# Hybrid encoder: the memory attention is issued after the first q tile, its values product in float32, and GpSimd makes the high parts of four w_out blocks

## The chip, the cores and the metric

The kernel runs on one core of one Trainium2 chip. The metric is the device time of one execution in microseconds. A core has a TensorE (PE, with its weight loads shown apart as PEld), a VectorE (DVE), a ScalarE (ACT), a GpSimd (POOL) and a SyncE (SP, which here issues most DMAs). Each engine works through its own instruction queue in order and waits on semaphores for the others.

## The reference

Two layers of an encoder on a sequence of 1024 rows of 1024 floats. In each layer three token mixers read one projection of the normed rows: a Fourier mixer, attention over a window of 128 to either side, and an attention of four heads over 256 memory rows. Their normed outputs go through `w_out`, and a gated feed-forward block follows.

```python
def _memory_attn(q, km, vm):
    scores = jnp.einsum('bshd,bmhd->bhsm', q, km).astype(jnp.float32) * (HEAD_DIM ** -0.5)
    probs = jax.nn.softmax(scores, axis=-1)
    return jnp.einsum('bhsm,bmhd->bshd', probs, vm).reshape(b, s, MEM_WIDTH)

for l in range(DEPTH):                                   # DEPTH = 2
    z = _rmsnorm(x, g_pre_mix[l]) @ w_in[l]              # (1024, 1024) @ (1024, 1280)
    zf, zq, zk, zv, zm = jnp.split(z, splits, axis=-1)   # 256, 512, 128, 128, 256
    y_f = _fourier_mix(zf, w_fourier[l])
    q = _rope(zq.reshape(b, s, 8, 64), positions)
    k = _rope(zk.reshape(b, s, 2, 64), positions)
    y_a = _window_attn(q, k, zv, sink[l])
    km, vm = jnp.split(_rmsnorm(mem, g_mem[l]) @ w_mem_kv[l], 2, axis=-1)   # 256 rows of memory
    y_m = _memory_attn(zm.reshape(b, s, 4, 64), km, vm)
    y = jnp.concatenate([_rmsnorm(y_f, ..), _rmsnorm(y_a, ..), _rmsnorm(y_m, ..)], -1) @ w_out[l]
    x = x + _rmsnorm(y, g_post_mix[l])
    gate, up = jnp.split(_rmsnorm(x, g_pre_ffn[l]) @ w_ffn_in[l], 2, axis=-1)
    x = x + _rmsnorm((jax.nn.silu(gate) * up) @ w_ffn_out[l], g_post_ffn[l])
```

The change touches the memory attention (`_memory_attn`) and the preparation of `w_out` for the product behind the three mixers.

## The kernel before, in words

**Products.** Nearly all matrix products are made in fp32r, with each operand split into a high part (a cast to fp32r, mostly on ACT) and a low part (what the cast left over, mostly a subtraction on DVE). A product is then three matmuls: high by high, high by low, low by high (`Acc.add`). `split` (L150 to L152) makes both parts of a tile.

**Memory.** Two large tiles are addressed in slots of 256 words per partition: `arena_r` for fp32r data and `arena_f` for float32, through `at(k, ...)`. `Ring` and `run` give several slots in turn. Weights that don't fit there lie in `big`, a pool of four buffers of 8 KB per partition. PSUM has four tags of two buffers each: `sc`, `pT`, `av`, `pd`.

**Stages of a layer's mixing part.** `zf` and the Fourier units; `kvz`, eight token tiles of 128 rows, that make keys, values and the memory queries (`zst`); `q`, eight token tiles: `q(t)` makes 24 matmuls of 512 columns (L162, tile `qp`) with the q weights, which fill the four `big` buffers, then the rotation (`rope`, DVE and POOL), and `q_turn(t)` transposes the result (L743, tile `qT`) and makes its high and low parts. `Memory.load` fetches the memory's keys and values, made earlier, from DRAM and splits them: `dup_stack` (L397 to L400) makes eight casts on ACT and eight subtractions on DVE for the keys.

**The memory attention** has 10 units for 8 pairs of a head and a half of the sequence. Unit i issues `mem_scores` of pair i: 16 matmuls of 256 columns (L873, tile `ms`), maxima on DVE (L875, L876), four exponentials on ACT (L879), a reciprocal on DVE (L883) and four multiplications on POOL (L885). It then issues `mem_values` of pair i - 2: four fp32r matmuls of 512 columns (L906, tile `mav`), whose 128 output rows are the 64 columns of the head by the high and by the low part of the values; ACT copies one half (L909) and DVE adds the other (L910). Last comes `mem_turn` of pair i - 1: eight transposes (L895, tile `mpT`) into two PSUM tiles, each split into high and low part (L151 on ACT, L152 on DVE).

**w_out.** `load_wout` takes eight raw blocks of 128 x 512 per call through a ring of three slots: a DMA (L942), the high part on ACT (L943), the low part on DVE (L944), for four row blocks. One call puts them into `big`, once the q weights are used up; the other puts them into `arena_r`. `fm_load` makes both, and `fm_units` the products of the Fourier and memory columns with them (tile `mo`, L162), whose sums go to DRAM until the last mixer is done. The windowed attention (`att_units`, tiles `sc`, `pT`, `av`) comes in two halves of the heads, and the second is woven with the rest of `w_out`. A feed-forward stage of Strassen-like blocks takes up the rest of the layer.

**Order.** The program is issued in the order of the Python code, where `weave` merges lists of units evenly; a scheduler then orders the instructions of each engine by their dependences and modelled times, so that the order on an engine isn't the order of the code. Buffers of pools may share memory where their uses don't overlap, and the later use waits for the earlier. In the main loop the q units 0 to 3 are issued first, then `mem.load()`, then the memory units woven with the q units 4 to 7, `fm_load` and the rest.

## Time and profile before

| what | value |
| --- | --- |
| median of 3 runs | 2080.04 us (2077.87 to 2081.79) |
| the profiled execution | 2080.67 us |
| its span, first to last instruction | 2078.9 us |
| mean granted TensorE clock | 0.981 |
| chain that ended last, by engine | PE 79%, DVE 7%, DMA 5%, ACT 3% |
| stage of the q tiles and the memory attention, layer 0 and layer 1 | 122.7 to 245 us, 1150.2 to 1260 us |

The span is that of one profiled execution, and all rows of the trace belong to it; its own time is 1.8 us longer, which lies outside the first and last instruction. The page gives busy shares over the whole span; the stage concerned is some 110 to 120 us long in each of the two layers. The slices of the page, each a fortieth of the span (52 us), show it as a dip of PE in slices 5 and 25, with DVE high at the same place:

```profile
PE   7998999799999999999999989998999999999998
PEld 6876787588888888887888768876888888878886
DVE  5668767898787886768876687679887787778766
```

A digit is the busy share of a slice in tenths. The trace also gives the busy times in any stretch, each engine's idle times with what ended them, and single instructions with start and length; rows of such views stand in the prediction.

### The profile page before, as it was taken

How to read it: one execution, taken by the hardware profiler on the slowest of the kernel's cores; microseconds unless marked ns; L12 is line 12 of the kernel's file. 1: busy time of each engine (PE TensorE's matmuls, PEld its weight loads, DVE VectorE, ACT ScalarE, POOL GpSimd, SP SyncE). 2: the span in 40 equal slices, each digit the busy share in tenths (PEclk: the TensorE clock that was granted, in tenths of full speed). 3: DMA queues.
4: the chain of work that ended last, by engine and by line, in shares of the span. 5: the costliest groups of instructions: out<-in, count | busy, mean ns of one | idle time of the engine just before them, and what ended most of it. 6: DMA issues, size and time to landing. Idle time of an engine off the chain costs nothing.

```text
span 2078.9 us, 28540 instructions
## 1 busy us (share of the span) xinstructions
PE 1996.4 (96%) x9587; PEld 1646.8 (79%) x9587; DVE 1572.7 (76%) x2540; ACT 1071.5 (52%) x2270; POOL 714.1 (34%) x819
## 2 busy tenths in 40 slices
PE   7998999799999999999999989998999999999998
PEld 6876787588888888887888768876888888878886
DVE  5668767898787886768876687679887787778766
ACT  7467777554333333545555677686433333345451
POOL 5344445433333433002423544453442342320012
PEclk9999999899999999999999999998999999999999
DMA  6112132423232333879741122233233233269983
GB/s 222 45 48 67 61 102 96 158 67 106 96 115 94 115 103 115 304 267 327 273 153 49 57 67 77 78 123 130 97 117 101 87 132 97 97 210 342 302 274 141
DMA packets 173347, 286.48 MB, mean 138 GB/s; under 512 B 15464, under 2 KB 73360, under 8 KB 173200
## 3 DMA queue, kind: packets, MB, share of 16 engines
q1 hardware_dynamic: 165136, 265.78, 38.4%
q10 hardware_dynamic: 8064, 18.88, 2.4%
q8 instruction: 75, 1.23, 0.2%
q14 instruction: 72, 0.59, 0.1%
HBM read 218.02 MB, written 66.58 MB: 137 GB/s over the span
## 4 chain that ended last, share of the span: by engine, by line
PE 79%; DVE 7%; DMA 5%; ACT 3%; issue 2%; POOL 2%; SPq 0%; DVEq 0%; POOLq 0%; ACTq 0%
PE fo L1272 14%; PE qx L1137 11%; PE qz L1137 11%; PE qy L1137 11%; PE mo L162 7%; PE qw L1137 6%; PE kvp L162 4%; PE qp L162 3%; DVE arena_r L152 2%; DMA arena_f<-actd 2%; PE pT L798 2%; PE zT L162 2%; PE sc L761 2%; DMA arena_f<-in_w_ffn_out 1%; PE av L813 1%
## 5 line engine op out<-in xcount | busy, mean ns | idle before, releaser
L151 ACT CAST arena_r<-arena_f 128x512 fp32r<-128x512 f32 (+1 forms) x780 | 443.8, 591 | 646.4 <-PE qz L1137 114.0
L152 DVE TENSOR_TENSOR arena_r<-arena_f,arena_r 128x512 fp32r<-128x512 f32 (+1 forms) x676 | 509.4, 775 | 146.3 <-ACT arena_r L151 136.4
L1272 PE MATMUL fo<-arena_r 128*128 128x512 f32 x1848 | 426.5, 392 | 8.1 <-ACT arena_r L151 6.9
L1272 PEld LDWEIGHTS fo<-arena_r 128*128 128x128 f32 x1848 | 347.9, 189 | 82.0 <-ACT arena_r L151 5.7
L1137 PE MATMUL qy<-arena_r 128*128 128x512 f32 x1056 | 261.6, 397 | 21.4 <-ACT arena_r L151 15.3
L1137 PEld LDWEIGHTS qy<-arena_r 128*128 128x128 f32 x1056 | 201.3, 192 | 66.1 <-ACT arena_r L151 16.4
L1127 DVE TENSOR_TENSOR arena_f<-arena_f 128x512 f32<-128x512 f32 x220 | 201.3, 920 | 11.5 <-DMA arena_f<-in_w_ffn_in 6.7
L1137 PE MATMUL qz<-arena_r 128*128 128x512 f32 x704 | 195.7, 389 | 0.2 <-ACT arena_r L151 0.2
L1157 POOL TENSOR_TENSOR arena_f<-arena_f 128x512 f32<-128x512 f32 x44 | 74.5, 1695 | 318.0 <-ACT arena_f L1142 318.0
L1137 PEld LDWEIGHTS qz<-arena_r 128*128 128x128 f32 x704 | 132.1, 188 | 28.0 <-ACT arena_r L151 0.6
L152 POOL TENSOR_TENSOR arena_r<-arena_f,arena_r 128x256 fp32r<-128x256 f32 (+2 forms) x104 | 86.3, 837 | 123.0 <-ACT arena_r L151 88.7
L1137 PE MATMUL qw<-arena_r 128*128 128x512 f32 x528 | 127.3, 389 | 0.0
L1137 PE MATMUL qx<-arena_r 128*128 128x512 f32 x528 | 127.3, 389 | 0.0
L1137 PE MATMUL qx<-big,arena_r 128*128 128x512 f32 x528 | 127.0, 389 | 0.0
L1189 POOL TENSOR_TENSOR arena_f<-arena_f 128x512 f32<-128x512 f32 x40 | 66.2, 1655 | 170.5 <-DVE arena_f L1169 127.1
L1137 PEld LDWEIGHTS qx<-arena_r 128*128 128x128 f32 x528 | 99.1, 188 | 20.6
L1137 PEld LDWEIGHTS qx<-big,arena_r 128*128 128x128 f32 x528 | 99.1, 188 | 20.6
L1137 PEld LDWEIGHTS qw<-arena_r 128*128 128x128 f32 x528 | 99.1, 188 | 20.6
L1137 PE MATMUL qz<-big,arena_r 128*128 128x512 f32 x352 | 115.2, 389 | 0.0
L210 POOL TENSOR_SCALAR rrsv<-rss 128x1 f32<-128x1 f32 x32 | 15.7, 492 | 268.1 <-ACT arena_f L323 208.6
L162 PE MATMUL mo<-big,arena_r 128*128 128x512 f32 x384 | 104.1, 410 | 0.7 <-ACT arena_f L1001 0.4
L162 PE MATMUL mo<-arena_r 128*128 128x512 f32 x384 | 100.5, 402 | 0.4 <-ACT arena_f L1001 0.3
(228 smaller groups left out, 3520.0 us busy)
## 6 DMA issues: line engine op xcount, KB each, us to landing
arena_f<-in_w_ffn_out SPq DMA_DIRECT2D x264, 256.0 KB, 4.7
arena_f<-in_w_ffn_in SPq DMA_DIRECT2D x88, 512.0 KB, 3.6
actd<-arena_f SPq DMA_DIRECT2D x154, 256.0 KB, 3.7
arena_f<-actd SPq DMA_DIRECT2D x154, 256.0 KB, 4.6
arena_f<-in_w_in SPq DMA_DIRECT2D x40, 256.0 KB, 2.9
arena_f<-in_x SPq DMA_DIRECT2D x16, 512.0 KB, 4.9
arena_f<-in_w_out SPq DMA_DIRECT2D x32, 256.0 KB, 2.8
pmd<-arena_f ACTq DMA_DIRECT2D x32, 256.0 KB, 2.0
```

The costliest lines, as they stand in the source:

```text
L151: nc.scalar.copy(hi, src)
L152: return (lo_eng or nc.vector).tensor_tensor(out=lo, in0=src, in1=f32(hi), op=ALU.subtract)
L162: mm(self.dst, a, b, start=self.i == 0, stop=self.i == self.n - 1)
L210: nc.gpsimd.tensor_scalar(out=v, in0=ss, scalar1=1.0 / n, scalar2=EPS, op0=ALU.mult, op1=ALU.add)
L761: mm(pt, lhs, self.kst[g][i][:, k0 * P : k1 * P], start=i == 0, stop=i == 1)
L798: nc.tensor.transpose(pT[:, h, :], es_[h // 2][:, h % 2, j * P : j * P + P], ident)
L813: mm(av, lhs, p_, start=j == 0 and i == 0, stop=j == nk - 1 and i == 1)
L1127: nc.vector.tensor_tensor(out=s, in0=a, in1=b, op=op)
L1137: mm(pt, a, b, start=start and n == 0, stop=n == 11, skip_group_check=not start)
L1157: nc.gpsimd.tensor_tensor(out=self.v, in0=self.v, in1=self.s2, op=ALU.add)
L1189: (G if i in (0, 3) else V).tensor_tensor(out=a[i], in0=c, in1=g[i], op=ALU.mult)
L1272: mm(pt, ab[:, 0, x, sl], ab[:, 1, y], start=new and first and j == 0, stop=last and j == 2, skip_group_check=not new)
```

## The change

Six edits:

- Slots 8 to 15 of the float32 arena become a tile of their own, `flex`, which is allocated anew as fp32r for the memory's keys when `mem.load()` is issued, and as float32 again when the windowed attention first writes its output there. Before, the keys lay in slots 16 to 23 of `arena_r`, where the normed rows of the first half lie until q tile 3 is done. The rings `es_ring` and `mps` get other slots.
- `mem.load` fetches keys and values in two DMAs; the values go straight to float32 slots and aren't split.
- `mem_turn` makes one float32 copy on ACT of each transposed tile in place of a high and a low part.
- `mem_values` works for a pair of heads: for each of two blocks of memory rows and each head one float32 matmul with 64 weight columns, into that head's half of the PSUM tile, and one copy on DVE. It is issued in units 3, 5, 7 and 9.
- `load_wout` fetches the left halves of its four row blocks before the right halves, and in the call into `big` POOL makes the high part.
- In the main loop only q unit 0 is issued ahead of `mem.load()`, and units 1 to 7 are woven with the memory units.

```diff
--- before.py
+++ after.py
@@ -88,8 +88,16 @@
 
     arenas = {
         F32R: cp.tile([P, ARENA_R * 256], F32R, name="arena_r"),
-        F32: cp.tile([P, ARENA_F * 256], F32, name="arena_f"),
+        F32: cp.tile([P, (ARENA_F - 8) * 256], F32, name="arena_f"),
     }
+    fxp = ctx.enter_context(tc.tile_pool(name="fxp", bufs=1))
+    flex = {}
+
+    def reflex(dt):
+        flex["t"] = fxp.tile([P, 8 * 256], dt, tag="flex", name=nm("flex"))
+        return flex["t"]
+
+    reflex(F32)
     bp = ctx.enter_context(tc.tile_pool(name="bp", bufs=4))
 
@@ -99,8 +107,11 @@
 
     def at(k, *shape, dt=F32):
 
+        t = arenas[F32R if dt is F32R else F32]
+        if dt is not F32R and k >= 8:
+            k, t = (k - 8, flex["t"]) if k < 16 else (k - 8, t)
         o = int(k * 256)
-        ap = arenas[F32R if dt is F32R else F32][:, o : o + math.prod(shape)]
+        ap = t[:, o : o + math.prod(shape)]
         return shaped(ap.bitcast(dt) if dt is I32 else ap, shape)
 
@@ -125,14 +136,14 @@
     raws, junks = run(0, 3, 2), Ring(56)
     yfs, turns, kvs, ds = run(8, 2, 1), Ring(32, 34), Ring(10, 56, 58), run(12, 2, 2)
     ropes = {2: run(6, 4, 0.5), 8: run(36, 6, 2)}
-    ems, es_ring, y1s = run(16, 4, 2), run(33, 5, 3), run(6, 2, 1)
+    ems, es_ring, y1s = run(16, 4, 2), Ring(36, 39, 42, 45, 33), run(6, 2, 1)
     sqs, pms, xfs = run(16, 2, 2), run(20, 2, 2), Ring(16, 20, 24, 28, 32, 0)
     qws, sns, silus, acts = Ring(32, 0, 16, 20), Ring(36, 38, 40, 42, 32, 34), run(8, 5, 2), run(18, 7, 2)
     sums, wsums = run(8, 4, 2), Ring(4, 6)
     ras, rbs, bsums, xs_ = run(40, 3, 2), run(46, 6, 2), Ring(58, 32, 34), Ring(36, 24)
 
     zzs, dhs, tabs = run(112, 2, 4), run(64, 2, 4), run(72, 4, 2)
-    mps, phs, yys = run(24, 2, 4), run(16, 3, 4), run(104, 2, 4)
+    mps, phs, yys = Ring(56, 58, 32, 34), run(16, 3, 4), run(104, 2, 4)
     wcs, abs_ = Ring(112, 116, 96, 100, 48, 52, 56, 60), Ring(80)
 
     def sm(n, name="v"):
@@ -471,16 +482,15 @@
             nc.sync.dma_start(kvd[self.l], at(self.ks, 1024))
 
         def load(self):
-            raw = at(32, 4, 256)
-            nc.sync.dma_start(raw, kvd[self.l].rearrange("p (i c) -> p i c", i=4))
-            self.km = [at(16 + 4 * i, 2, 2, NMEM, dt=F32R) for i in range(2)]
-            self.vm = at(120, 2, 4, 2, HD, dt=F32R)
+            raw = at(32, 2, NMEM)
+            nc.sync.dma_start(raw, kvd[self.l, :, 0:512].rearrange("p (i c) -> p i c", i=2))
+            self.v = at(6, 2, 4, HD)
+            nc.sync.dma_start(self.v, kvd[self.l, :, 512:1024].rearrange("p (t h d) -> p t h d", t=2, h=4))
+            km = shaped(reflex(F32R), (2, 2, 2, NMEM))
+            self.km = [km[:, i] for i in range(2)]
             for ci in range(2):
                 for j in range(2):
                     dup_stack(self.km[ci][:, j, 0], self.km[ci][:, j, 1], raw[:, ci], j)
-            v = raw[:, 2:4].rearrange("p t (h d) -> p t h d", h=4)
-            for mt in range(2):
-                split(self.vm[:, mt, :, 0, :], self.vm[:, mt, :, 1, :], v[:, mt])
 
 
     class Mix:
@@ -844,6 +854,7 @@
                     n = i - SKEW
                     half, c = divmod(n, 4)
                     if g == 0 and n == 0:
+                        reflex(F32)
                         ya = at(8, 2, 2, 512)
                         self.ya[0, 0], self.ya[0, 1] = ya[:, 0], ya[:, 1]
                     if g == 0:
@@ -893,21 +904,17 @@
                 pT = ps([4, P], "mpT", "pT")
                 for b in range(4):
                     nc.tensor.transpose(pT[:, b, :], e[b // 2][:, b % 2, mt * P : mt * P + P], ident)
-                pp = mps(2, 512, dt=F32R)
-                split(pp[:, 0], pp[:, 1], pT.rearrange("p h q -> p (h q)"))
-                res.append((pp[:, 0], pp[:, 1]))
+                pf = mps(512)
+                nc.scalar.copy(pf, pT.rearrange("p h q -> p (h q)"))
+                res.append(pf)
             return res
 
-        def mem_values(self, h, half, pp):
+        def mem_values(self, pr, half, pfs):
             av = ps([512], "mav", "av")
             for mt in range(2):
-                lhs = self.mem.vm[:, mt, h].rearrange("p a d -> p (a d)")
-                for i in range(2):
-                    mm(av, lhs, pp[mt][i], start=mt == 0 and i == 0, stop=mt == 1 and i == 1)
-            s = h % 2
-            d = self.ym[half][64 * s : 64 * s + 64, h // 2, :]
-            nc.scalar.copy(d, av[64:128])
-            nc.vector.tensor_tensor(out=d, in0=av[0:64], in1=d, op=ALU.add)
+                for s in range(2):
+                    mm(av[64 * s : 64 * s + 64], self.mem.v[:, mt, 2 * pr + s], pfs[s][mt], start=mt == 0, stop=mt == 1)
+            nc.vector.tensor_copy(self.ym[half][:, pr, :], av)
 
         def mem_units(self):
             todo = [(h, half) for half in range(2) for h in range(4)]
@@ -917,34 +924,35 @@
             def unit(i):
                 if i < n:
                     st[i] = self.mem_scores(*todo[i])
-                if i >= 2:
-                    h, half = todo[i - 2]
-                    if h == 0 and half == 0:
+                if i >= 3 and i % 2:
+                    h, half = todo[i - 3]
+                    if i == 3:
                         ym = at(24, 2, 2, 512)
                         self.ym = [ym[:, i] for i in range(2)]
-                    self.mem_values(h, half, pp.pop(i - 2))
+                    self.mem_values(h // 2, half, [pp.pop(i - 3), pp.pop(i - 2)])
                 if 1 <= i <= n:
                     pp[i - 1] = self.mem_turn(st.pop(i - 1))
 
             return [lambda i=i: unit(i) for i in range(n + 2)]
 
-
         def load_wout(self, ks, k0=None):
 
-            res = {}
-            for j, k in enumerate(ks):
-                w = big(2, D) if k0 is None else at(k0 + 8 * j, 2, D, dt=F32R)
-                hi, lo = w[:, 0], w[:, 1]
-                g = ggT[:, self.l * NK + k : self.l * NK + k + 1]
-                for n in range(2):
-                    ns = slice(n * 512, n * 512 + 512)
+            w = [big(2, D) if k0 is None else at(k0 + 8 * j, 2, D, dt=F32R) for j in range(len(ks))]
+            res = {k: (w[j][:, 0], w[j][:, 1]) for j, k in enumerate(ks)}
+            for n in range(2):
+                ns = slice(n * 512, n * 512 + 512)
+                for k in ks:
+                    hi, lo = res[k]
+                    g = ggT[:, self.l * NK + k : self.l * NK + k + 1]
                     raw = raws(512)
                     nc.sync.dma_start(raw, T["w_out"][self.l, k * P : (k + 1) * P, ns])
-                    nc.scalar.activation(hi[:, ns], raw, AF.Copy, scale=g)
+                    if k0 is None:
+                        nc.gpsimd.tensor_scalar(out=hi[:, ns], in0=raw, scalar1=g, scalar2=1.0, op0=ALU.mult, op1=ALU.mult)
+                    else:
+                        nc.scalar.activation(hi[:, ns], raw, AF.Copy, scale=g)
                     nc.vector.scalar_tensor_tensor(
                         out=lo[:, ns], in0=raw, scalar=g, in1=f32(hi[:, ns]), op0=ALU.mult, op1=ALU.subtract
                     )
-                res[k] = (hi, lo)
             return res
 
         def group_scale(self, parts, n, ring):
@@ -1364,10 +1372,9 @@
         kvz = mix.skewed(mix.kvz, mix.kvz_turn, NT)
         weave(mix.fourier_units(), kvz[:8] + [mix.q_load] + kvz[8:])
         q = mix.skewed(mix.q, mix.q_turn, NT)
-        for u in q[:4]:
-            u()
+        q[0]()
         mem.load()
-        weave(mix.mem_units(), q[4:8] + [mix.fm_load] + q[8:])
+        weave(mix.mem_units(), q[1:8] + [mix.fm_load] + q[8:])
         fm = mix.fm_units(pmd)
         weave(mix.att_units(0), fm[:6] + [mix.out_load] + fm[6:])
         mix.out_gains()
```

What this does to the order of the instructions is shown at three places, all in layer 0. A row is a line, an operation, the tile written and the tiles read, with the number of that allocation, the shape and a count of equal neighbours. Code lines of the changed program are some ten higher: L173 is L162, L884 is L873, L906 is L895, L408 to L411 are L397 to L400, and L952 and L953 are L943 and L944.

PE before, at the first scores of the memory attention; `qp_1497`, `qp_1598` and `qp_1728` are the q tiles 3, 4 and 5, `big_1305` to `big_1329` the four buffers with the q weights, `ms` the scores:

```order
L162 MATMUL qp_1497<-big_1329,arena_r 128x512 x6
L162 MATMUL qp_1598<-big_1305,arena_r 128x512 x3
L873 MATMUL ms_1571<-arena_r 128x256 x3
L873 MATMUL ms_1580<-arena_r 128x256 x3
L162 MATMUL qp_1598<-big_1305,arena_r 128x512 x3
L162 MATMUL qp_1598<-big_1313,arena_r 128x512 x2
L743 MATMUL qT_1529<-const,arena_f 128x128 x4
L162 MATMUL qp_1598<-big_1313,arena_r 128x512 x4
L162 MATMUL qp_1598<-big_1321,arena_r 128x512 x6
L162 MATMUL qp_1598<-big_1329,arena_r 128x512 x6
L162 MATMUL qp_1728<-big_1305,arena_r 128x512 x4
```

PE of the changed program, at its first scores; `qp_1889` and `qp_1969` are q tiles 6 and 7, `big_1309` to `big_1333` the q weights, `flex_1421` the keys:

```order
L173 MATMUL qp_1889<-big_1325,arena_r 128x512 x6
L173 MATMUL qp_1889<-big_1333,arena_r 128x512 x6
L173 MATMUL qp_1969<-big_1309,arena_r 128x512 x6
L173 MATMUL qp_1969<-big_1317,arena_r 128x512 x6
L173 MATMUL qp_1969<-big_1325,arena_r 128x512 x6
L173 MATMUL qp_1969<-big_1333,arena_r 128x512 x6
L884 MATMUL ms_1450<-flex_1421,arena_r 128x256
L884 MATMUL ms_1459<-flex_1421,arena_r 128x256
L884 MATMUL ms_1450<-flex_1421,arena_r 128x256 x3
L884 MATMUL ms_1459<-flex_1421,arena_r 128x256 x3
L884 MATMUL ms_1521<-flex_1421,arena_r 128x256 x4
L884 MATMUL ms_1530<-flex_1421,arena_r 128x256 x4
```

Before, the first scores stand among the products of q tile 4, and the products of tiles 5 to 7 follow. In the changed program all eight q tiles stand ahead of the first scores. The memory of `flex_1421` is that of `big_1333`, the last quarter of the q weights, which is read until the last product of q tile 7. Layer 1 has the same order.

ACT of the changed program, where the keys' high parts (L408, L409) are made; L417 are the high parts of q, L952 those of `w_out`, L890 the exponentials:

```order
L417 CAST arena_r<-qT_1589 64x4x128
L417 CAST arena_r<-qT_1669 64x4x128 x2
L408 CAST flex_1421<-arena_f 64x256
L409 CAST flex_1421<-arena_f 64x256
L408 CAST flex_1421<-arena_f 64x256
L409 CAST flex_1421<-arena_f 64x256
L408 CAST flex_1421<-arena_f 64x256
L409 CAST flex_1421<-arena_f 64x256
```

```order
L162 CAST arena_r<-arena_f 128x256
L952 ACTIVATE arena_r<-arena_f,const 128x512
L890 ACT_TABLE_LOAD
L890 ACTIVATE arena_f,den_1449<-ms_1450,nmx_1445 128x256 x2
L890 ACTIVATE arena_f,den_1449<-ms_1459,nmx_1445 128x256 x2
L952 ACTIVATE arena_r<-arena_f,const 128x512 x2
```

DVE of the changed program, at the keys' low parts (L410, L411) and the first maxima (L886); L681 and L683 are rotations of q tiles, L953 low parts of `w_out`:

```order
L681 TENSOR_TENSOR arena_f<-qp_1803,ct_1828 128x512
L683 TENSOR_TENSOR arena_f<-qp_1803,st_1829 128x512
L953 SCALAR_TENSOR_TENSOR big_2056<-arena_f,const,big_2056 128x512
L953 SCALAR_TENSOR_TENSOR big_2057<-arena_f,const,big_2057 128x512
L953 SCALAR_TENSOR_TENSOR big_2058<-arena_f,const,big_2058 128x512
L953 SCALAR_TENSOR_TENSOR big_2055<-arena_f,const,big_2055 128x512
L410 TENSOR_TENSOR flex_1421<-arena_f,flex_1421 64x256
L411 TENSOR_TENSOR flex_1421<-arena_f,flex_1421 64x256
L410 TENSOR_TENSOR flex_1421<-arena_f,flex_1421 64x256
L411 TENSOR_TENSOR flex_1421<-arena_f,flex_1421 64x256
L953 SCALAR_TENSOR_TENSOR big_2056<-arena_f,const,big_2056 128x512
L410 TENSOR_TENSOR flex_1421<-arena_f,flex_1421 64x256
```

Before, the keys' casts and subtractions (L397 to L400) stand among the Fourier units and the first q tiles, and no low part of `w_out` ahead of the first maxima. Now the casts stand behind the high parts of q tiles 0 to 2 on ACT, and four low parts of `w_out` stand ahead of the first subtraction of a key on DVE.

## The prediction

> **What bounds the kernel now.** I read the page first, then busy time by stage, then TensorE's waits, then the timeline of the memory attention. The page says that TensorE (PE) is the bound.
>
> ```profile
> span 2078.9 us, 28540 instructions
> PE 1996.4 (96%) x9587; PEld 1646.8 (79%) x9587; DVE 1572.7 (76%) x2540; ACT 1071.5 (52%) x2270; POOL 714.1 (34%) x819
> ```
>
> An average hides the few stages where it isn't. The stages below run from the first q product; the first five rows are layer 0, the next four layer 1. The columns are busy us and, in brackets, instructions of PE, PEld, DVE, ACT and POOL; then the granted clock, the DMA share and GB/s.
>
> ```profile
> 122.70:150.00 27.30, 25.02 (x113) 20.23 (x112) 13.88 (x23) 14.38 (x36) 14.13 (x20) 0.94 0.17 49
> 150.00:182.90 32.90, 32.90 (x183) 28.25 (x182) 26.49 (x51) 20.38 (x56) 13.81 (x24) 1.00 0.05 16
> 182.90:212.00 29.10, 20.62 (x96) 15.54 (x96) 27.25 (x50) 23.13 (x60) 15.03 (x21) 0.82 0.32 101
> 212.00:229.30 17.30, 15.02 (x69) 12.21 (x68) 14.24 (x51) 14.40 (x44) 7.97 (x15) 0.80 0.04 16
> 229.30:245.00 15.70, 15.70 (x89) 13.25 (x88) 9.74 (x28) 11.52 (x29) 7.38 (x13) 1.00 0.15 44
> 1150.20:1171.30 21.10, 18.10 (x85) 14.22 (x84) 11.67 (x20) 18.13 (x49) 13.42 (x20) 0.92 0.26 82
> 1171.30:1213.80 42.50, 42.50 (x227) 36.10 (x227) 32.15 (x61) 22.51 (x58) 17.45 (x30) 1.00 0.08 26
> 1213.80:1246.50 32.70, 23.17 (x107) 16.65 (x105) 29.24 (x51) 25.58 (x67) 14.09 (x21) 0.84 0.27 89
> 1246.50:1260.00 13.50, 12.74 (x66) 9.71 (x67) 11.89 (x42) 11.51 (x32) 6.74 (x14) 1.00 0.05 19
> ```
>
> While q products remain (150 to 182.9) PE is full although units of the memory attention run between them. Once they are used up (182.9 to 212), PE is idle 8.48 us and the granted clock falls to 0.82, while DVE is 94% busy. So the q products are the filler of this attention, and after them DVE (with ACT) sets the pace. What PE waits for in it:
>
> ```profile
> PE mpT L895 <- POOL arena_f L885: 7.4, 6, 3.0
> PE ms L873 <- ACT arena_f L879: 4.0, 2, 2.1
> PE mav L906 <- ACT arena_r L151: 3.0, 3, 1.6
> PE mav L906 <- DVE arena_r L152: 2.0, 2, 1.8
> ```
>
> **What the change takes from the engines.** Prices of one instruction, from the groups by line:
>
> ```profile
> L152 DVE TENSOR_TENSOR arena_r<-mpT,arena_r 128x512 fp32r<-128x512 f32 x32 | 21.2, 683 | 3.4 <-ACT arena_r L151 3.2
> L151 ACT CAST arena_r<-mpT 128x512 fp32r<-128x512 f32 x32 | 17.6, 589 | 2.6 <-PE mav L906 1.4 <-PE mpT L895 0.9
> L910 DVE TENSOR_TENSOR arena_f<-mav,arena_f 64x512 f32<-64x512 f32 x16 | 10.9, 683 | 1.4 <-ACT arena_f L909 1.0
> L909 ACT COPY arena_f<-mav 64x512 f32<-64x512 f32 x16 | 9.3, 583 | 10.2 <-PE mav L906 9.9
> L943 ACT ACTIVATE big<-arena_f,const 128x512 fp32r<-128x512 f32 x16 | 11.1, 725 | 12.6 <-DMA arena_f<-in_w_out 6.6 <-PE qp L162 5.8
> L342 POOL TENSOR_SCALAR arena_f<-arena_f,const 128x512 f32<-128x512 f32 x16 | 15.5, 970 | 27.0 <-DMA arena_f<-in_w_in 26.0 <-issue 0.6
> L944 DVE SCALAR_TENSOR_TENSOR arena_r<-arena_f,const,arena_r 128x512 fp32r<-128x512 f32 x16 | 14.1, 905 | 1.4 <-ACT arena_r L943 1.3
> L885 POOL TENSOR_SCALAR arena_f<-arena_f,rden 128x256 f32<-128x256 f32 x64 | 34.1, 552 | 42.3 <-DVE rden L883 26.9 <-DVE nmx L876 15.4
> ...
> arena_f<-in_w_out SPq DMA_DIRECT2D x32, 256.0 KB, 2.8
> ```
>
> Per layer DVE loses 16 low parts of the transposed weights (10.9 us) and 8 folds (5.5), and gains 4 copies of a 128x512 product. No such copy is in the trace: from ACT's 0.58 to DVE's 0.68, I take 0.68, 2.7 in all. DVE: 13.7 us less. ACT keeps 16 copies (cast or copy, 0.59), loses 8 copies (4.7) and 8 high parts (5.8): 10.5 less. POOL gains these 8; nearest row 0.97, upper end 1.4; 7.8 us on an engine with room (8 to 15 busy of every 17 to 30 us). The split of the memory's values (4 instructions of about this size) goes too. The second small load of it is issued long before its use: nothing, or at most the 2.8 us of one load.
>
> PE's values products: 8 x 4 fp32r ones become 4 x 4 float32 ones of 64 columns. The timeline has both kinds (start, us, instructions):
>
> ```profile
> 182.86 1.09 PE L906 MATMUL mav<-arena_r 128*128 128x512 f32 x4
> 183.79 0.63 PE L873 MATMUL ms<-arena_r 128*128 128x256 f32 x4
> ...
> 317.64 0.60 PE L806 MATMUL av<-big,arena_f 128*64 128x256 f32 x4
> 318.17 0.62 PE L761 MATMUL sc<-arena_r 128*128 128x384 f32 x2
> ...
> 319.06 0.65 PE L806 MATMUL av<-big,arena_f 128*64 128x256 f32 x4
> 319.64 2.57 PE L162 MATMUL mo<-arena_r 128*128 128x512 f32 x10
> ```
>
> Four of before take 0.93 until the next product starts (183.79), 0.23 each, so 7.5 per layer. Four av records are two float32 products over 256 columns; the next product starts 0.53 to 0.58 later, so 512 columns cost 1.06 to 1.16 a pair, and 8 pairs 8.5 to 9.3: 1 to 2 us more PE work per layer, where PE has slack; I take 0. The Trainium skill ("FP8 and Floating Point Precision", TensorE Precision Notes) gives true FP32 four passes through the array. Without sharing between the two column halves that would be 15 us per layer in place of 9; the av rows (0.53 to 0.58 for two products over 256 columns) don't bear it out, and the sum goes without it.
>
> If this were all, each layer would gain part of its 8.48 us of idle time and of the slow clock. It isn't all.
>
> **What the change moves.** The order of the changed program (above) has all eight q tiles ahead of the first ms product on PE, in both layers. The new key tile has been put where the last quarter of the q weights lies, so ACT's first write to it waits for the last product of q tile 7. "Begins with the second tile" does not happen; the attention loses the filler that it had. I follow layer 0 by hand, from E, the start of the last q product.
>
> ```profile
> 145.98 5.51 PE L162 MATMUL qp<-big,arena_r 128*128 128x512 f32 x23
> 167.36 1.19 PE L873 MATMUL ms<-arena_r 128*128 128x256 f32 x8
> 168.63 1.03 PE L895 MATMUL mpT<-const,arena_f 128*128 128x128 f32 x8
> 155.73 0.48 ACT L879 ACTIVATE arena_f<-ms,nmx 128x256 f32<-128x256 f32 x1
> 157.09 0.48 ACT L879 ACTIVATE arena_f<-ms,nmx 128x256 f32<-128x256 f32 x1
> 211.66 0.47 ACT L879 ACTIVATE arena_f<-ms,nmx 128x256 f32<-128x256 f32 x1
> 1245.92 0.47 ACT L879 ACTIVATE arena_f<-ms,nmx 128x256 f32<-128x256 f32 x1
> ```
>
> *q stage.* 192 products x 0.233 ((5.51 - 0.39) / 22) = 44.7, some 18 transposes x 0.11 = 2.0, 0.8 of small waits: E = 122.7 + 47.5 = 170.2. The 2.28 us of idle time in 122.7 to 150 belong to a product that waits for a PSUM buffer which it need not wait for in the new order, so they go.
>
> *First unit.* ACT's 8 key copies (about 0.41) start at E. On DVE, ahead of the first key's low part, stand four w_out low parts (0.74 at best), the last not before E+2.5, since its raw block reuses a buffer freed at E-2.3 (its load takes 2.8 and POOL 0.97). 8 key low parts (0.42) and one more w_out part: E+6.6. Two maxima (0.64): 7.9. Two more w_out parts: 9.4. Scaling: 9.7. Then four exponentials, 0.45 apart (155.73 to 157.09 is three of them): E+11.9.
>
> *Seven more units.* On ACT each has 4 exponentials (2.0 with their tail), 2 copies (1.1), a seventh of 8 q casts (0.66) and one w_out high part (0.73): 4.5; DVE has some 4.3. Both are in-order queues that wait for each other, for POOL's four multiplications (2.2) and for the three-buffer chain of w_out loads (2.8 + 0.73 + 0.74 each round), so I take 5.0: the last unit's exponentials end at E + 11.9 + 35 = E + 47 = 217.2. Before, they ended at 212.1 (211.66 + 0.47): **5.1 us later**. Before, the last four units took 5.6 each from 190, with more DVE work; 4.5 to 6.0 are the bounds, so 213.7 to 224.2, or +1.6 to +12.
>
> The matmuls issued by these two moments are nearly the same (all scores, 12 mo products), so the lag carries over. Behind it, before loses 2.28 us to idle time and 0.20 x 17.3 = 3.5 to the clock in 212 to 229.3; the change puts 12 mo products ahead of the first pT transposes, worth up to 2.8, and a longer cold start may take it back: 0, from -4 to +3.
>
> *Layer 1.* q starts at 1150.2; 44.7 + 2.0 + 24 Fourier products x 0.12 = 2.9, and about 4.3 of idle time and slow clock in its first row, whose cause (ACT, 18.13 busy of 21.1) stays: E = 1204.1, last exponentials 1251.1 against 1246.4: **4.7 us later**.
>
> **Sum.** +5.1 + 4.7 = +9.8 on the profiled execution's 2080.67 us (span 2078.9 and 1.8 around it; the median of the three runs shown is 2080.04, so the two are alike): 2090.5, say 2091. The feed-forward order is unchanged, so nothing is booked there.
>
> **Rivals.**
>
> 1. *The lighter engines win.* If ACT runs without gaps, a unit is 4.3 and the start 10: 40 in place of 47, 2 us ahead of before, and with the mo products 5 us ahead per layer: 2071 to 2076. For it: 13.7 and 10.5 us less work. Against: DVE was 94% busy before only because nothing was queued behind late loads. 0.20, with 0.02 in it for the attention starting early after all, which would free most of the 19 us per layer lost in 182.9 to 229.3 (2050); PE's order speaks against that.
> 2. *Even.* Units at 4.6 and 2 us back behind them: 2077 to 2084. 0.18.
> 3. *The clock stays low.* In the new stage PE has 24 us of work in 47 (8 units x 0.95 for scores and 0.87 for transposes, three values pairs, 12 mo products), in bursts with gaps. At half clock that is 48 us, PE is late at each hand-over, and the stage takes about 57: +10 per layer on top, 2110. It decides from the point at which gaps keep the clock down for most of the stage; before, with 20.62 of 29.1 busy, the mean was 0.82, so about a third. 0.14. The Trainium skill ("TensorE: Matmul & The Clock Gate", What's actually happening) says that the clock halves after an idle window of about 3.4 us and comes back after as long a busy one. By that the bursts here would hardly ever bring it back, and 2110 would follow; the trace agrees in kind (1.00 in every full row above, 0.80 to 0.84 in the broken ones), not in degree.
>
> **Numbers.** Forecast 2091, 2084 to 2103: 0.48. Slower is that case and the third: 0.62; same 0.18; faster 0.20. 0.2%, 4.2 us, is about what a measurement of this kernel tells from no change. The range for 8 in 10 reaches into rivals 1 and 3: 2074 to 2107.
>
> **What would show it.** Right: no ms product ahead of q tile 7's last; PE full from 122.7 to about 170, then a stage of 45 to 50 us with PE half idle, ACT and DVE some 80 to 90% busy, the last exponential about 217 and 1251; mpT low parts gone; POOL's w_out parts near 1 us. Wrong: a stage under 42 us, float32 pairs far above 1.2 us, a clock near 0.5 throughout it, or a difference that comes from outside the two mixing stages.

## The result, and the profile after

The changed kernel takes 2104.95 us (median of 4 runs, 2103.63 to 2107.37) where the kernel before took 2080.05 in the same session: ratio 1.0123, 95% interval 1.0108 to 1.0138. That is 24.9 us slower, where 11 had been forecast. The profiled execution took 2104.46 us (span 2102.6). The page of the changed kernel, in the lines that answer to those of before (span, busy times, and the slices):

```profile
span 2102.6 us, 28477 instructions
PE 2012.1 (96%) x9587; PEld 1641.3 (78%) x9587; DVE 1553.8 (74%) x2496; ACT 1052.7 (50%) x2234; POOL 725.3 (34%) x835
...
PE   7997999799999999999999979997999999999998
PEld 6885787578888888787888748775888888878886
DVE  5656667887787877678866576679878778778866
```

DVE and ACT have each lost about 19 us of busy time (27.4 and 21.0 had been forecast), and the kernel is still slower. PE's digits in slices 4, 24 and 28 have fallen from 8 to 7 (the dips at the memory attention are in slices 4 and 24, not 5 and 25 as said above): the memory attention of both layers, at 158 to 210 and 1209 to 1262 us, and 1419 to 1472 us, where the feed-forward part of layer 1 begins. The stages of the changed kernel, with columns as in the prediction; the first three rows are layer 0 (q tiles, memory attention, what follows), the next three layer 1, the last the entry into layer 1's feed-forward part. The row below them is that entry in the kernel before:

```profile
123.00:169.20 46.20, 46.14 (x214) 37.72 (x212) 21.05 (x32) 12.49 (x31) 21.71 (x33) 1.00 0.16 46
169.20:218.70 49.50, 37.71 (x173) 23.99 (x173) 36.01 (x75) 37.27 (x107) 25.67 (x40) 0.79 0.18 59
218.70:235.00 16.30, 15.87 (x84) 11.44 (x84) 11.88 (x45) 12.05 (x35) 7.27 (x14) 1.00 0.09 34
...
1158.40:1209.40 51.00, 48.78 (x233) 39.92 (x231) 24.84 (x39) 17.81 (x44) 25.38 (x38) 1.00 0.16 53
1209.40:1259.10 49.70, 37.10 (x171) 23.73 (x170) 38.53 (x77) 38.32 (x107) 25.29 (x40) 0.79 0.19 59
1259.10:1276.00 16.90, 16.65 (x91) 12.59 (x92) 10.59 (x43) 12.67 (x38) 9.07 (x17) 1.00 0.19 63
...
1435.00:1466.50 31.50, 19.46 (x66) 13.70 (x65) 28.90 (x45) 16.45 (x29) 10.33 (x7) 0.78 0.30 102
```

```profile
1417.40:1446.70 29.30, 19.36 (x77) 14.18 (x76) 28.57 (x45) 16.43 (x30) 7.01 (x7) 0.77 0.41 134
```

Two stages have the same face. In the memory attention PE is busy 37.7 of 49.5 us at a clock of 0.79. The prediction had foreseen such a stage, with PE half idle and DVE and ACT 80 to 90% busy; here PE is busy 76%, DVE 73% and ACT 75%. At the entry into the feed-forward part PE is busy 19.46 of 31.5 at 0.78, and DVE 28.9. That stage was slow before too (19.36 of 29.3 at 0.77), but now it is longer, and the prediction had booked nothing there.

To see where the 24 us arise, the two traces are laid beside each other at equal PE work. Each product of PE counts with the median interval that its kind (tile, shape) takes in the trace of before; the memory's values products, which differ, are left out. The lag is how much later than before a kernel has done the work that before had done at a mark. The marks, in before's time: 122 (first q product), 250 (windowed attention running), 390 (last tile's products), 500 (feed-forward), 1150, 1260, 1430, 1460. A row shows by how much the lag grew between two marks. Each row is one execution. Equal code differs between executions by 4.3 us ahead of the first mark (the change and e1) and by up to 2.6 in a column (e4 and e7 in mixing 0, where their order is that of before). In the later sessions the kernel before took 2082 to 2084 us, so ratios are compared, not times.

| kernel | up to 122 | mixing 0 | window 0 | entry 0 | ffn 0 | mixing 1 | window 1 | entry 1 | rest | lag at the end |
| --- | --- | --- | --- | --- | --- | --- | --- | --- | --- | --- |
| the change | 0.4 | 2.3 | 1.0 | 3.6 | 0.9 | 5.8 | 1.1 | 9.2 | -0.6 | 23.7 |
| e1 entry order | 4.7 | 2.8 | 1.0 | -2.7 | -1.7 | 10.3 | 1.1 | 3.5 | -0.6 | 18.4 |
| e2 early start | 3.3 | -9.7 | 5.4 | 3.9 | 0.8 | -4.3 | 2.8 | 2.1 | 1.3 | 5.6 |
| e3 both | 2.1 | -6.9 | 5.4 | -0.3 | -2.0 | -3.7 | 1.3 | 4.7 | 2.4 | 3.0 |
| e4 entry in before | 0.7 | -2.4 | -0.1 | 6.2 | -1.0 | 0.9 | 1.1 | 8.0 | 2.3 | 15.7 |
| e5 float32 values | 2.4 | -6.3 | 2.0 | -0.7 | -3.5 | -0.1 | 1.5 | 9.3 | 0.4 | 5.0 |
| e6 POOL's high parts | -0.3 | 3.8 | 0.3 | -3.1 | -1.7 | 1.7 | 1.1 | 9.8 | 1.2 | 12.8 |
| e7 order in before | 0.4 | -2.6 | -0.1 | -1.6 | -0.5 | 1.6 | 0.3 | 4.7 | 1.0 | 3.2 |
| e8 paired products | 1.5 | -14.4 | -1.6 | -0.1 | 0.8 | -2.3 | 0.7 | 1.8 | 0.3 | -13.3 |
| e9 float32, paired | 1.6 | -9.8 | -0.5 | -2.4 | 1.2 | -0.3 | 0.1 | 7.5 | -1.1 | -3.7 |
| e10 paired, late start | 3.0 | 5.9 | 0.2 | 1.3 | -1.0 | 6.6 | 1.0 | 3.5 | -0.8 | 19.7 |

In the changed kernel the two mixing stages cost 2.3 + 5.8 = 8.1 us and the two entries 3.6 + 9.2 = 12.8. The mark at 1430 lies inside the entry of layer 1, which begins where the last output products end, at 1417. Counted from there, "entry 1" is 7.6 for the change and the two entries 11.2; it is 6.9 to 8.1 for e4, e5 and e6, and 0.6 to 4.1 for all others. What is taken off there belongs to "window 1".

**The entry of layer 1.** PE of the kernel before; `mo` are the last output products of the mixing part, `hTp` the transposes of the normed rows, `qy` and `qz` the first feed-forward products:

```profile
1415.40 2.11 PE L162 MATMUL mo<-arena_r 128*128 128x512 f32 x8
...
1434.99 3.49 PE L1137 MATMUL qy<-arena_r 128*128 128x512 f32 x14 [0.68 <-ACT arena_f L1142]
1438.36 0.64 PE L1066 MATMUL hTp<-const,arena_f 128*128 128x128 f32 x4
1439.67 0.66 PE L1066 MATMUL hTp<-const,arena_f 128*128 128x128 f32 x4 [0.68 <-ACT big L1067]
1440.08 2.57 PE L1137 MATMUL qy<-arena_r 128*128 128x512 f32 x10
...
1446.69 3.56 PE L1137 MATMUL qz<-arena_r 128*128 128x512 f32 x15
```

The same in the changed kernel:

```profile
1433.00 2.11 PE L173 MATMUL mo<-arena_r 128*128 128x512 f32 x8
...
1449.86 3.48 PE L1145 MATMUL qy<-arena_r 128*128 128x512 f32 x14 [0.68 <-ACT arena_f L1150]
1455.15 4.15 PE L1145 MATMUL qy<-arena_r 128*128 128x512 f32 x10 [1.81 <-DVE arena_r L163]
1459.98 3.04 PE L1145 MATMUL qy<-arena_r 128*128 128x512 f32 x12 [0.68 <-ACT arena_f L1150]
1462.86 0.60 PE L1074 MATMUL hTp<-const,arena_f 128*128 128x128 f32 x4
1464.13 0.66 PE L1074 MATMUL hTp<-const,arena_f 128*128 128x128 f32 x4 [0.68 <-ACT big L1075]
1466.50 0.73 PE L1145 MATMUL qz<-arena_r 128*128 128x512 f32 x2 [1.71 <-ACT arena_r L162]
1467.83 0.73 PE L1145 MATMUL qx<-arena_r 128*128 128x512 f32 x2 [0.60 <-ACT arena_r L162]
1469.59 5.60 PE L1145 MATMUL qz<-arena_r 128*128 128x512 f32 x17 [1.03 <-DVE arena_r L163]
```

From the last mo to the last transposes it is 24.3 us before and 31.1 after. The last tile's transposes release most of what follows, and they now stand behind 22 more qy products that wait for their own operands. Behind the transposes these 22 products are then missing: before goes on with qy at 1440.08, while the changed kernel has PE idle for 1.71, 0.60 and 1.03 us until the last tile's rows are split. DVE's residual and norm of the last tile are late too. DVE of the changed kernel, then of before, at the addition of the last mo (L1049, L1041) and the end of the norm (L305, L294); the first two rows are sums that stand ahead of the addition:

```profile
1435.52 0.68 DVE L1092 TENSOR_TENSOR flex<-big,big 128x512 f32<-128x512 f32 x1
1436.13 0.68 DVE L1104 TENSOR_TENSOR big<-big,big 128x512 f32<-128x512 f32 x1
...
1442.13 1.40 DVE L1049 SCALAR_TENSOR_TENSOR arena_f<-mo,grs,arena_f 128x512 f32<-128x512 f32 x2
1458.83 1.28 DVE L305 SCALAR_TENSOR_TENSOR arena_f<-arena_f,nrs 128x1024 f32<-128x1024 f32 x1 [0.72 <-POOL nrs L223]
```

```profile
1419.84 1.39 DVE L1041 SCALAR_TENSOR_TENSOR arena_f<-mo,grs,arena_f 128x512 f32<-128x512 f32 x2
1436.93 1.29 DVE L294 SCALAR_TENSOR_TENSOR arena_f<-arena_f,nrs 128x1024 f32<-128x1024 f32 x1 [0.73 <-POOL nrs L212]
```

The addition comes 2.3 us behind the last product's end before (1419.84 less 1417.51) and 7.0 after (1442.13 less 1435.11): sums for later blocks stand ahead of it on DVE. From the addition to the norm's end it is 18.4 us before and 18.0 after. The transposes start 2.8 us after the norm's end, 0.1 before. 4.7 - 0.4 + 2.6 make up the 6.9 us by which 31.1 exceeds 24.3.

### The profile page after: what moved, and what is told of

It reads as the page before. It is cut to its first block, busy times and chain, and to the rows that moved or that the text cites. A ratio compares the mean times of both kernels' runs of the same rounds, so it can differ in the third digit from the quotient of the medians.

```text
span 2102.6 us, 28477 instructions
## 1 busy us (share of the span) xinstructions
PE 2012.1 (96%) x9587; PEld 1641.3 (78%) x9587; DVE 1553.8 (74%) x2496; ACT 1052.7 (50%) x2234; POOL 725.3 (34%) x835
## 4 chain that ended last, share of the span: by engine, by line
PE 79%; DVE 6%; POOL 5%; issue 4%; ACT 3%; DMA 3%; POOLq 0%; DVEq 0%; SPq 0%; ACTq 0%
PE fo L1280 18%; PE qz L1145 11%; PE qx L1145 11%; PE qy L1145 10%; PE mo L173 6%; PE qw L1145 6%; PE kvp L173 4%; PE zT L173 2%; PE qp L173 2%; PE sc L771 2%; DVE arena_r L163 2%; PE pT L808 2%; DMA arena_f<-actd 1%; POOL arena_f L795 1%; PE av L823 1%
## 5 line engine op out<-in xcount | busy, mean ns | idle before, releaser
L162 ACT CAST arena_r<-arena_f 128x512 fp32r<-128x512 f32 (+2 forms) x714 | 411.6, 598 | 625.4 <-PE qz L1145 126.3
L163 DVE TENSOR_TENSOR arena_r<-arena_f,arena_r 128x512 fp32r<-128x512 f32 x632 | 475.9, 774 | 144.4 <-ACT arena_r L162 135.3
L1135 DVE TENSOR_TENSOR arena_f<-arena_f 128x512 f32<-128x512 f32 x220 | 204.4, 934 | 8.8 <-DMA arena_f<-in_w_ffn_in 3.9
L1165 POOL TENSOR_TENSOR arena_f<-arena_f 128x512 f32<-128x512 f32 x44 | 70.9, 1613 | 316.2 <-ACT arena_f L1150 316.2
L173 PE MATMUL mo<-arena_r 128*128 128x512 f32 x384 | 100.7, 402 | 0.2 <-DVE arena_f L1049 0.2
L173 PE MATMUL mo<-big,arena_r 128*128 128x512 f32 x384 | 100.5, 399 | 0.0
L1197 POOL TENSOR_TENSOR arena_f<-arena_f,flex 128x512 f32<-128x512 f32 x32 | 52.5, 1640 | 137.4 <-DVE arena_f L1177 101.5
L1261 DVE TENSOR_TENSOR arena_f<-arena_f 128x512 f32<-128x512 f32 x110 | 81.1, 739 | 20.9 <-DMA arena_f<-in_w_ffn_out 19.3
```

The source lines that it names most:

```text
L162: nc.scalar.copy(hi, src)
L163: return (lo_eng or nc.vector).tensor_tensor(out=lo, in0=src, in1=f32(hi), op=ALU.subtract)
L173: mm(self.dst, a, b, start=self.i == 0, stop=self.i == self.n - 1)
L1135: nc.vector.tensor_tensor(out=s, in0=a, in1=b, op=op)
L1165: nc.gpsimd.tensor_tensor(out=self.v, in0=self.v, in1=self.s2, op=ALU.add)
L1197: (G if i in (0, 3) else V).tensor_tensor(out=a[i], in0=c, in1=g[i], op=ALU.mult)
```

## The experiments

Theory A: the loss has two parts that don't depend on each other, the late start of the memory attention and the order in which the feed-forward part is entered, which the scheduler sets and which any change ahead of it can tip. Theory B: all of it is the late start, passed on. Theory C: the float32 product or POOL's parts cost it. The seven runs e1 to e7 were set against these.

**e1, the entry's order alone**, in the changed kernel. What the feed-forward part issues late keeps its place behind the last tile's addition (a place in the order only, no wait). PE's order follows: 24 qy products stand between the transposes of the last two tiles, where the changed kernel has 46:

```diff
-                nc.vector.scalar_tensor_tensor(
+                self.last = nc.vector.scalar_tensor_tensor(
...
+            with tc.issue_after(mix.last.ins) if i > NT + 1 else nullcontext():
                 if i == NT + 2:
                     gq.step(4)
...
+        with tc.issue_after(mix.last.ins):
             for q in first:
                 q.step(5)
```

> The changed kernel, where DVE and PE may take up the feed-forward blocks that are issued late (the second product pair and what follows it) only behind the residual of the last token tile; nothing else differs, and the memory attention still starts behind all q products. Theory A (the order in which the feed-forward part is entered costs about 3 us in layer 0 and 9 us in layer 1, by itself): about 2094 us, 2090 to 2098, and the lag behind the kernel before at equal PE work no longer grows by 9 us between 1430 and 1450 us. Theory B (the loss at the entry is only the late start of the memory attention, passed on): 2105 us, within 2.

2098.88 us, ratio 1.0076 (1.0061 to 1.0091): about 10 us less than the change's 1.0123, and just above the 2090 to 2098 of A. The entries went from 3.6 to -2.7 and from 9.2 to 3.5. Only part of it reached the end: in layer 1 the tie upstream also moved rows of the mixing stage, which lost 10.3 instead of 5.8; layer 0's order up to the entry is the same row for row. B falls: the start was as late as ever.

**e4, the entry's order alone, in the kernel before**, the other way round: PE takes the last tile's transposes only behind the second pair's products.

```diff
...
+                if i == NT + 3:
+                    with tc.issue_after(lastmm[0].ins):
+                        hb.tile(hs.pop(i - 4), i - 4)
...
```

> The kernel before, where PE may take the last tile's transposes at the entry into the feed-forward part only behind the second pair of products, as the changed kernel does; the mixing stages are untouched. Theory A: slower, by 4 to 12 us in the two layers (2084 to 2092). Theory B: 2080 us, within 2. If only DVE's order counts and PE's doesn't, also 2080 us, and e1 decides between the two.

2096.25 us, ratio 1.0064 (1.0039 to 1.0090): 13 us lost in a kernel whose attention starts early, more than the 4 to 12 expected. The entries cost 6.2 and 8.0. DVE and PE of this run, the last addition, the end of the last norm and the transposes that need it:

```profile
1425.32 1.40 DVE L1041 SCALAR_TENSOR_TENSOR arena_f<-mo,grs,arena_f 128x512 f32<-128x512 f32 x2
...
1441.28 1.28 DVE L294 SCALAR_TENSOR_TENSOR arena_f<-arena_f,nrs 128x1024 f32<-128x1024 f32 x1
```

```profile
1421.91 2.11 PE L162 MATMUL mo<-arena_r 128*128 128x512 f32 x8
...
1441.74 8.66 PE L1139 MATMUL qy<-arena_r 128*128 128x512 f32 x24 [2.88 <-ACT arena_f L1144]
1451.08 3.03 PE L1139 MATMUL qy<-arena_r 128*128 128x512 f32 x12 [0.68 <-ACT arena_f L1144]
1453.94 0.60 PE L1066 MATMUL hTp<-const,arena_f 128*128 128x128 f32 x4
```

The rows are ready at 1442.56 and PE turns to them at 1453.94, 11.4 us later. Theory A's mechanism is shown: no work was changed, only one place in PE's queue. In layer 0 all engines keep the order of before up to 415 us; at the entry DVE and ACT then get another order too, and in layer 1 some rows of the mixing stage move. DVE's last addition is not late in this run (1425.32, 1.3 us behind the end of the last mo product), so PE's place alone is enough for such a loss. What DVE's late addition (the 4.7 us above) adds in the changed kernel stays open.

**e2, an early start in the changed kernel.** POOL's high parts for `big` are tied behind POOL's multiplications of the memory attention's first unit. Then no `big` buffer takes the old place of `flex` early, and the keys get that place instead of the last quarter of the q weights.

```diff
-                        nc.gpsimd.tensor_scalar(out=hi[:, ns], ...)
+                        with tc.issue_after(self.p0.ins):
+                            nc.gpsimd.tensor_scalar(out=hi[:, ns], ...)
```

> The changed kernel, where POOL's high parts of w_out for the shared buffers are queued behind POOL's first multiplication of the memory attention. They then don't take the old place of the flexible tile early, the keys get that place, and the first scores come after two to three q tiles (48 and 71 q products) in place of 192. By its order the entry into the feed-forward part stays as in the changed kernel in layer 0 and is that of the kernel before in layer 1. Theory A (late start and entry order are two separate losses): the mixing stages lose their 8 us and gain up to 8 more by the lighter DVE, layer 1's entry gives back 8 to 9: 2078 us, 2072 to 2088. Theory B (all of the loss is the late start): 2070 us or less. Theory C (the float32 product or POOL's parts are what costs): above 2092 us, as much as the changed kernel less a few us.

2088.24 us, ratio 1.0018 (1.0001 to 1.0035), at the upper end of A's range of 2072 to 2088. The first scores of this run on PE:

```profile
139.67 0.50 PE L884 MATMUL ms<-flex,arena_r 128*128 128x256 f32 x2 [1.76 <-ACT flex L409]
```

The scores came at 139.67 us instead of 170.33, the mixing stages went from +2.3 and +5.8 to -9.7 and -4.3, and layer 1's entry, in before's order, from 9.2 to 2.1. Layer 0's, in the changed order, stayed at 3.9. But the windowed attention behind gave 5.4 and 2.8 back, so that the lighter engines brought nothing at the end. C is excluded as the main cause: the float32 products and POOL's parts are all in this run.

**e3, both edits.**

> Both edits of the two runs before: early start, and the entry into the feed-forward part held behind the last tile's residual. Theory A: some 3 us less than e2_early_start (layer 0's entry), 2075 us, 2068 to 2083, below the kernel before. Theory B: the same as e2_early_start within 2 us. Theory C: above 2090 us.

2083.59 us, ratio 1.0007 (0.9989 to 1.0026): layer 0's entry fell from 3.9 to -0.3 as expected, layer 1's rose to 4.7 (the tie has a price where the order was right), and the total is that of before, 8 us above what was expected. The change as it was meant, with both faults mended, is worth nothing in this form.

**e5, the float32 values alone, in the kernel before** (the new `mem_turn`, `mem_values` and value loads; keys, start and `load_wout` as before; slots of two rings as in the change).

> The kernel before with one part of the change alone: values in float32, one copy of each transposed tile, four float32 products for a pair of heads, values loaded apart. Keys, start and w_out as before; the first scores stand behind 42 and 44 q products. By its order the entry into the feed-forward part has the changed kernel's form in layer 1 (46 qy products ahead of the last transposes) and one near that of before in layer 0. Theory A (entry order and late start are two separate losses): the mixing stages gain 2 to 8 us by the lighter DVE, layer 1's entry loses 8: about 2085 us, 2080 to 2090 where before is 2082, and the loss stands at the entry of layer 1. Theory B (all loss comes from the late start): 2078 us or less. If the float32 products are what costs, the loss stands in the memory attention instead.

2088.25 us, ratio 1.0025 (1.0012 to 1.0038). The mixing stages gain 6.3 and 0.1, and layer 1's entry, in the changed kernel's order, loses 9.3. So a kernel that arrives there early loses as much as one that arrives late.

**e6, POOL's high parts alone, in the kernel before** (the new `load_wout`).

> The kernel before with another part alone: load_wout of the changed kernel (POOL's high parts in the shared buffers, left halves first). Start as before (38 and 48 q products ahead of the first scores). Entry of layer 1 in the changed kernel's form, that of layer 0 between the two. Theory A: mixing stages within 3 us of before, the entries lose 2 and 8: 2092 us, 2086 to 2097. Theory B: 2082 us, within 3.

2094.00 us, ratio 1.0049 (1.0034 to 1.0064). The sum was expected, the places only in part: layer 1's entry lost 9.8, but layer 0's mixing lost 3.8 and its entry gained 3.1.

**e7, e1's tie in the kernel before.**

> The kernel before with the edit of e1_entry_order (feed-forward blocks that are issued late stay behind the last tile's residual on DVE and PE). Its order there was near this already (hTp ahead of the second pair's products). Theory A: within 4 us of before, 2078 to 2086; the tie brings nothing where the order was right. If the tie itself makes DVE wait, slower by over 4 us at the two entries, and what e1_entry_order won is a lower bound.

2088.27 us, ratio 1.0018 (1.0006 to 1.0030), 4 us: the tie costs 4.7 at layer 1's entry (2.3 from 1417) and gains 1.6 at layer 0's, together less than the 4 us named as the sign of a wait. What e1 won may be a lower bound; that isn't shown.

Across the runs, layer 1's entry costs 8.0 to 9.8 us in the four kernels whose order there holds 46 qy products between the transposes of the last two tiles (the change, e4, e5, e6), and 1.8 to 4.7 in the six whose order holds about 24 there (e1, e2, e3, e7, e8, e10); from 1417 it is 6.9 to 8.1 and 0.6 to 4.1. The start was early in three of the first four and late in two of the six. e9 is in neither group.

**e8 and e9, the float32 products side by side.** In the changed kernel the products of two heads mostly stand apart. PE of the changed kernel, two rows and the start of the next of each:

```profile
205.86 1.08 PE L916 MATMUL mav<-arena_f 128*64 128x512 f32 x4
206.87 0.77 PE L906 MATMUL mpT<-const,arena_f 128*128 128x128 f32 x5
207.56 1.07 PE L916 MATMUL mav<-arena_f 128*64 128x512 f32 x2
208.57 0.74 PE L884 MATMUL ms<-flex,arena_r 128*128 128x256 f32 x4
```

One product (two records) takes 1.01 us, and two products of different heads take the same 1.01 together. The edit issues the four of a pair one behind the other, the last operand first:

```diff
+            p = None
-            for mt in range(2):
-                for s in range(2):
-                    mm(av[64 * s : 64 * s + 64], ..., start=mt == 0, stop=mt == 1)
+            for mt in (1, 0):
+                for s in (1, 0):
+                    with tc.issue_after(p.ins) if p is not None else nullcontext():
+                        p = mm(av[64 * s : 64 * s + 64], ..., start=mt == 1, stop=mt == 0)
```

> e3_early_and_order with the four float32 products of a pair of heads issued one behind the other, the one whose operand comes last first. In e3 they stand apart and take 14.9 and 14.4 us of PE per layer; two of different heads side by side took 1.01 us together, one alone 1.01 as well. Side by side they should take 8 to 10 us per layer. If PE is what ends there (it was busy 45.9 of 49.5 us at full clock in that stretch of e2_early_start): 4 us per layer less than e3, ratio to before 0.997, 0.995 to 1.000. If DVE and ACT end there all the same: as e3, 1.0007 within 0.002.

2066.16 us, ratio 0.9906 (0.9887 to 0.9924): faster than both kernels, and by more than expected. PE of e8 shows the four products of a pair in 1.87 us (193.84 to 195.71):

```profile
193.84 1.94 PE L918 MATMUL mav<-arena_f 128*64 128x512 f32 x8
195.71 0.44 PE L906 MATMUL mpT<-const,arena_f 128*128 128x128 f32 x2
```

By such intervals the products take 7.6 and 9.2 us per layer, in e3 12.9 and 14.1 (idle time in them left out; with it 14.9 and 14.4, as in the expectation). That is 10 us, and the lag falls by 16. But the places don't answer to this: layer 0 gains 7.5 in the mixing stage and 7.0 in the windowed attention, which no longer gives 5.4 back, while layer 1's mixing stage gains nothing (-2.3 for -3.7), and what layer 1 does gain lies behind it. PE's order moved from the first pairs on, so how much of the 16 us is the pairing's own stays open.

> e5_float32_values with the same pairing and with the entry into the feed-forward part held behind the last tile's residual as in e1_entry_order. Keys, start and w_out as before. By e5 the mixing stages are 6 us ahead of before and layer 1's entry loses 9; with the entry's order mended that loss should fall to 2 to 5 us, and pairing takes another 0 to 4 us: ratio 0.997, 0.994 to 1.000. If the loss at the entry comes of the lighter mixing stages and not of the order: 1.0025 as e5.

2077.46 us, ratio 0.9962 (0.9949 to 0.9975). The total came as expected. Of the place this can't be said: layer 1's entry lost 7.5 by the table, but 4.0 counted from 1417, where 2 to 5 had been expected. Its order there is a third form, with the last transposes in two parts behind 14 and 24 qy products, in spite of the tie.

**e10, pairing alone in the changed kernel.**

> The changed kernel with the four float32 products of a pair of heads side by side, nothing else; late start as in the changed kernel (192 q products first). By its order layer 1's entry into the feed-forward part has the form of before, layer 0's a form like the changed kernel's. The products should take 8 to 9 us of PE per layer in place of 12.8. PE has idle time in the memory attention, so this should bring little there, 0 to 3 us per layer, and layer 1's entry 7 to 9: ratio 1.006, 1.004 to 1.009. If the mixing stage shrinks by 5 us or more per layer, the products standing apart were part of the loss: 1.001 to 1.004.

2098.02 us, ratio 1.0065 (1.0044 to 1.0086). The products fell to 9.1 and 9.2 us, and the mixing stages got no shorter (5.9 and 6.6). With the late start PE waits there anyway; what it gains over the change is at layer 1's entry, 3.5 for 9.2 (4.1 for 7.6 from 1417). So the separated products were no visible part of the loss, and pairing paid where PE was nearly full (e8), not here.

## Why the prediction was right in its direction and too small

The measured 2104.95 us lies above the range of 2084 to 2103, and inside the wide one of 2074 to 2107.

**Right: the late start and its cause, and its size in part by luck.** No scores came ahead of q tile 7's last product. ACT's first key cast waited for that product. Before, the first scores were earlier still than said above: the order shown there as that of the first scores is the one at 151.32 us, and two single score products had come at 131.84 and 133.11, behind 38 and 42 q products. PE of before, then PE and ACT of the changed kernel:

```profile
131.84 0.36 PE L873 MATMUL ms<-arena_r 128*128 128x256 f32 x1
...
151.32 0.88 PE L873 MATMUL ms<-arena_r 128*128 128x256 f32 x6
```

```profile
149.37 20.00 PE L173 MATMUL qp<-big,arena_r 128*128 128x512 f32 x87
170.33 0.51 PE L884 MATMUL ms<-flex,arena_r 128*128 128x256 f32 x2 [0.96 <-ACT flex L409]
```

```profile
169.45 0.40 ACT L408 CAST flex<-arena_f 64x256 fp32r<-64x256 f32 x1 [17.89 <-PE qp L173]
180.27 0.48 ACT L890 ACTIVATE arena_f<-ms,nmx 128x256 f32<-128x256 f32 x1
218.19 0.47 ACT L890 ACTIVATE arena_f<-ms,nmx 128x256 f32<-128x256 f32 x1
1258.64 0.48 ACT L890 ACTIVATE arena_f<-ms,nmx 128x256 f32<-128x256 f32 x1
```

E was forecast at 170.2 and came at 169.0. The first unit's exponentials ended 11.8 us later (forecast 11.9), the last at 218.7 (217.2): a further unit took 5.4 us, within the bounds, where 5.0 had been taken. In layer 1 they ended 100.7 us behind the first q product at 1158.4, and 100.9 had been forecast. That this fits so well is luck: E came after 50.7 us instead of 53.9, and the stage behind it took 49.9 instead of 47. e2 confirms the cause.

**Right in sum, not in its parts: the lag carried over.** In layer 0, 6.5 us at the last exponential (6.1 without the 0.4 from the start) shrank to 2.3 by 250 us, within the bound of -4 given; in layer 1, 4.5 net grew to 5.8. Together 8.1, where 9.8 were forecast.

**Wrong, and the step that failed: "The feed-forward order is unchanged, so nothing is booked there."** The order well inside the feed-forward part is the same, but at its entry it isn't, in either layer: the last tile's transposes had moved behind the second pair's qy products, and sums had moved ahead of the last addition on DVE. That costs 12.8 us by the table, 11.2 with layer 1 counted from 1417. e4 shows that such an order costs as much in a kernel whose work is unchanged (6.2 and 8.0), and e1 shows it from the other side. The prediction itself had named a difference from outside the two mixing stages as a sign of being wrong. It overlooked that a change upstream can tip the scheduler's order downstream: e5 and e6, which don't touch the entry in the code either, got the same order in layer 1.

**Mis-sized: the float32 products.** The prediction took 1.06 to 1.16 us for a pair, and measured is 1.01, but only some came in pairs, so 12.8 and 12.4 us per layer instead of 8.5 to 9.3. It cost nothing here (e10), since PE waited. The sentence on the Trainium skill ("FP8 and Floating Point Precision", TensorE Precision Notes) would have given 15: four passes hold for a product that stands alone (1.01 us against 4 x 0.23 = 0.92), and two heads side by side share them.

**The rivals.** The clock did not stay low: 0.79 in the memory attention, and the stage took 49.7 us from E where 47 had been forecast and 57 in that rival. The rule of the Trainium skill ("TensorE: Matmul & The Clock Gate", What's actually happening), which as the prediction applied it would have given 2110, came nearer to the total for another reason, and the trace does not agree in degree with a clock that hardly ever comes back. That the lighter engines win was out of reach while the start was late. With the early start (e2) the mixing stages were 14 us ahead; the windowed attention and the entries took it back.

**Other prices.** Copy of a product on DVE 0.69 us (forecast 0.68); POOL's high part 0.79 (0.97). The DVE groups that went and the one that came differ by 27.3 us in all, as forecast (27.4), but DVE's busy time fell by 18.9 only; why stays open. Groups by line of the changed kernel:

```profile
L950 POOL TENSOR_SCALAR big<-arena_f,const 128x512 fp32r<-128x512 f32 x16 | 12.7, 793 | 17.2 <-PE qp L173 10.2 <-DMA arena_f<-in_w_out 5.5 <-PE yfT L592 1.3
...
L917 DVE COPY arena_f<-mav 128x512 f32<-128x512 f32 x8 | 5.5, 692 | 6.7 <-PE mav L916 6.7
```

## What to carry to other kernels

Where a scheduler sets the order, read the changed program at every place at which the bound engine has no slack, above all at the seams between stages, and not only where the edit lies; compare the rows there one by one before a term is set to nothing. A buffer that is "made free" earlier helps only if its new place isn't in use: look up what lies at the address that the first writer waits for. A tie that forces one order is cheap to try, in both directions, and tells a loss by order from a loss by work.

## What the runs showed of the hardware that was not expected

Two float32 products with 64 weight columns each, in different column halves and next to each other in the queue, take 1.01 us together, about as the prediction had it. That one alone takes 1.01 as well it had not. With other work between them the pair costs 2.0. In the kernel with an early start, where PE was busy 38.84 of 41 us (e3, 169 to 210 us), putting them side by side took 5.2 and 4.9 us off these products per layer (e8), and this kernel was faster than either original (0.9906), though not all of that is shown to be the pairing's.
